# The first weights' transfers on ScalarE's queue, their first half split by ScalarE and VectorE

## The chip, the core and the metric

The kernel runs on one core of one Trainium2 chip. The metric is the device time of the whole program in microseconds (us), less is better. TensorE (PE) does the matmuls and transposes, VectorE (DVE), ScalarE (ACT) and GpSimd (POOL) the elementwise work, SyncE (SP) issues most transfers. All transfers of the core go through 16 DMA engines.

## What is computed

A trunk of two layers over 1024 tokens of width 1024. Cut to what matters here, each layer is:

```python
for l in range(DEPTH):                       # DEPTH = 2
    h = rms_norm(x, norm_g[l])
    proj = h @ w_in[l]                       # [1024, 1024] @ [1024, 2504]
    (qa, ka, va, iq, ik, iw, ga, u, gb, cq, ckv, kpe, gc) = jnp.split(proj, points, axis=-1)
    # three mixers (sparse attention, state-space layer, latent attention), gated
    x = x + mixed @ w_out[l]
```

Only the start of the first layer is touched by the change: the load of x, its norm, and the first of the column groups of `w_in[0]`, the one that gives `ka`, `va`, `ik` and `iw` (128 + 40 + 32 = 200 columns).

## The kernel before

Every matmul operand is held as two fp32r tiles, high part and rest (hi and lo), and a product is three matmuls: hi·hi, hi·lo, lo·hi (lines 758, 760 and 761). Tokens go in eight tiles of 128, named x0 to x7 below, and in two halves (`hf` 0 and 1: x0 to x3, x4 to x7).

Line 703 on, the start: for each token tile a transfer of 512 KB is issued on SP (line 705). After the fourth tile come the constants (line 708), the gains (`load_gains`, lines 671 and 674) and `ws.load(2)`, the first two weight requests: request K for rows 0 to 511 of `w_in` (`kh` 0) and rows 512 to 1023 (`kh` 1). `wload` (line 625) issues one transfer per column range, and K has three ranges (128, 40 and 32 columns), so these are six transfers of 256, 80, 64, 256, 80 and 64 KB, each in 512 rows of 512, 160 or 128 bytes. The names w1 to w6 are used for them below. Then x4 to x7 follow.

`norm_tile` (line 659) takes the squares on ScalarE (line 663), the power −0.5 on GpSimd (`rsq`, lines 162 and 163) and scales on VectorE (line 666). `normed[0]` is the last of these powers. `turn_h` (line 677) transposes four tokens' blocks on TensorE (line 685), takes the high part out of PSUM on ScalarE (line 688, tile `hh`) and the rest on VectorE (line 689, tile `hl`). At line 727 the two weight tiles are split by `split_pool`: high part (line 149) and rest (line 150) on GpSimd, both for 800 columns a partition; `issue_after(normed[0])` holds those of the block's instructions that are on GpSimd behind the last power. `split_act` (line 152) is the other splitter: high part on ScalarE (line 153), rest on the engine that it is given (line 154); it does the splits of all later weights. `proj_halves` (line 737) is the first user: it gets both weight tiles, multiplies tokens x0 to x3 by `kh` 0 and then by `kh` 1 (48 matmuls each), then transposes x4 to x7 and multiplies these.

The order in which each engine runs its instructions is fixed when the program is built: a planner walks the traced program with a timeline of its own and gives each engine, SP included, one queue that runs strictly in order. Where two are ready by the planner's timeline, the one traced earlier goes first. A transfer is an instruction in the queue of the engine that issues it.

Of the kernel before, what the change touches and what calls it, by code (L numbers as in the profile page):

```python
# [86 lines left out]
def hybrid_kernel(ctx, tc, A, out, dbg=None, layers=DEPTH):  # L87
    nc = tc.nc
    V, S, G, T = nc.vector, nc.scalar, nc.gpsimd, nc.tensor
# [9 lines left out]
    def page(shape, dt, name):  # L99
        return pg.tile(shape, dt, tag="pg", name=name)  # L100
# [29 lines left out]
    def f(ap):  # L130
        return ap.bitcast(F32)
# [20 lines left out]
    def split_act(raw, hi, lo, eng=None):  # L152
        S.activation(hi, raw, AF.Copy)  # L153
        (eng or G).tensor_tensor(lo, raw, f(hi), op=ALU.subtract)  # L154
# [444 lines left out]
    class Stream:  # L599
# [20 lines left out]
        def get(self):  # L620
            self.load(LOADS[len(self.reqs) < 9])
            self.split(SPLITS[len(self.reqs) < 9])
            return self.q.pop(0)

    def wload(src, ranges, kh):

        raw = page([128, 4, 256], F32, "raw")
        o = 0
        for c0, c1 in ranges:
            nc.sync.dma_start(raw[:, :, o:o + c1 - c0],  # L630
                              src[512 * kh:512 * kh + 512, c0:c1].rearrange("(k p) c -> p k c", p=128))
            o += c1 - c0
        return raw, o

# [9 lines left out]
    def in_weights(l):  # L644
        cols = dict(K=R_K, I=R_IQ, L=R_L, C=R_CQ, Q=R_QA)
        reqs = []
        for x in "KI" + STEPS:
            if x.isdigit():
                reqs.append(lambda col=GATES[int(x)]: gate_w(l, col))
            elif x == "U":  # L650
                reqs.extend(lambda col=col: gate_w(l, col) for col in (1192, 1320))
            else:
                reqs.extend(lambda r=cols[x], kh=kh: wload(A["w_in"][l], r, kh) for kh in range(2))
        return Stream(reqs)
# [4 lines left out]
    def norm_tile(xt):  # L659

        jk = page([128, 1024], F32, "jk")
        ssq = small(1, "ssq")
        S.activation(jk, xt, AF.Square, accum_out=ssq)
        rst = small(1, "rst")
        normed[0] = rsq(rst, ssq, 1024 * EPS, 1.0 / 1024)
        V.tensor_scalar(jk, xt, rst, None, op0=ALU.mult)
        return jk

    def load_gains(l):
        gp = sm.tile([128, 11], F32, tag="gp", name="gp", bufs=2)  # L670
        nc.sync.dma_start(gp, A["gain_p"][l])
        gr = sm.tile([128, 320], F32, tag="gr", name="gr", bufs=1)
        src = A["gain_r"][l]
        nc.sync.dma_start(gr, bass.AP(tensor=src.tensor, offset=src.offset, ap=[[0, 128], [1, 320]]))
        return gp[:, 0:8], gp[:, 8:10], gp[:, 10:11], gr[:, 0:64], gr[:, 64:128], gr[:, 128:224], gr[:, 224:320]
# [25 lines left out]
    ws = in_weights(0)  # L701
    xnew = []
    for t in range(8):
        xp = page([128, 1024], F32, f"x{t}")
        nc.sync.dma_start(xp, A["x"][0][128 * t:128 * t + 128, :])
        xnew.append(xp)
        if t == 3:
            nc.sync.dma_start(cst_, A["c_all"])
            gains = load_gains(0)
            ws.load(2)  # L710
    htok = [norm_tile(x) for x in xnew[0:4]]
    hT = [[], []]
    turnh = turn_h(0, hT, htok, gains[0])
# [6 lines left out]
    for l in range(layers):  # L720
# [3 lines left out]

        if l == 0:
            with tc.issue_after(normed[0]):
                ws.split(2, split_pool)
        for _ in turnh:
            pass
        h_hi, h_lo = hT  # L730
# [831 lines left out]
        for g in range(2):  # L1562
            if g == 1 and not last:
                ws = in_weights(l + 1)
# [7 lines left out]
            for t in range(8):  # L1572
                cs = slice(128 * t, 128 * t + 128)
                ps = ps_s([128, 512], "po")
                for k in range(8):
                    hi, lo = (w[:, k % 2, :] for w in w_[k // 2][:2])
# [85 lines left out]
```

## Time and profile before

| what | time or share |
|---|---|
| three runs, median (lowest to highest) | 1314.76 us (1314.67 to 1316.2) |
| the profiled execution | 1314.69 us |
| its span | 1312.9 us |
| TensorE busy | 1229.4 us, 94% |
| VectorE, ScalarE, GpSimd busy | 67%, 52%, 52% |
| mean granted TensorE clock | 0.975 of full speed |

The span runs from the first to the last instruction of the profiled execution; the rest of its time lies around it. Times of rows are counted from the span's start. Busy shares are means over the whole program, so what the change is worth is read from the first 40 us alone.

### The profile page before, as it was taken

To read this page: it belongs to the slowest core of one execution; us is meant where nothing else is said; L and a number is where in the kernel's file an instruction comes from. 1 tells how busy PE (TensorE), PEld (TensorE's weight loads), DVE (VectorE), ACT (ScalarE), POOL (GpSimd) and SP (SyncE) were. 2 spreads that over 40 slices of the span, in tenths; PEclk is the share of its full clock that TensorE was granted. 3 is DMA by queue.
4 is the path that set the end of the run, shared out by engine and by line. 5 is a ranking of instruction groups with operands and counts; after the bars stand their busy time and mean duration, and the time that the engine had idled before them with its cause. 6 is when DMAs were issued, how large, how long until landed. Compare 5 with 4: busy or idle time off the path is not lost. (4 is left out here: it accounts for less than half of the span.)

```text
span 1312.9 us, 23852 instructions
## 1 busy us (share of the span) xinstructions
PE 1229.4 (94%) x8644; PEld 1047.7 (80%) x8644; DVE 876.9 (67%) x2342; ACT 686.5 (52%) x1565; POOL 681.0 (52%) x1112
## 2 busy tenths in 40 slices
PE   6898999698999999999999999996989999999998
PEld 6896998487788688877899888975868886887787
DVE  4968889926787787632253887997476879776111
ACT  5256753022778788752143666412157887777300
POOL 5789159767332556313247962795680345643300
PEclk8998999898999999999999999998989999999999
DMA  7011322322300100331140013223303010014102
GB/s 243 15 42 33 103 91 85 113 76 93 86 19 17 43 27 18 108 139 42 80 148 14 21 61 97 73 93 106 117 27 97 7 59 17 12 38 168 70 33 96
DMA packets 78491, 92.79 MB, mean 71 GB/s; under 512 B 13536, under 2 KB 61280, under 8 KB 78368
## 3 DMA queue, kind: packets, MB, share of 16 engines
q1 hardware_dynamic: 77216, 87.03, 20.7%
q0 software_dynamic: 1152, 4.19, 1.0%
q8 instruction: 68, 1.11, 0.4%
q14 instruction: 55, 0.45, 0.1%
HBM read 63.53 MB, written 26.50 MB: 69 GB/s over the span
## 5 line engine op out<-in xcount | busy, mean ns | idle before, releaser
L758 PE MATMUL pj<-whi,hh 128*128 128x256 f32 (+1 forms) x608 | 173.8, 286 | 1.2 <-POOL whi L149 1.2
L760 PE MATMUL pj<-wlo,hh 128*128 128x256 f32 (+1 forms) x608 | 172.6, 284 | 1.6 <-POOL wlo L150 1.6
L761 PE MATMUL pj<-whi,hl 128*128 128x256 f32 (+1 forms) x608 | 172.7, 285 | 0.0
L154 POOL TENSOR_TENSOR wlo<-raw,whi 128x1024 fp32r<-128x1024 f32 (+1 forms) x40 | 96.0, 2412 | 144.0 <-ACT whi L153 123.9
L166 PE MATMUL gt<-hh,whi 128*128 128x512 f32 x320 | 130.7, 408 | 0.0
L168 PE MATMUL gt<-hh,wlo 128*128 128x512 f32 x320 | 129.1, 405 | 0.0
L167 PE MATMUL gt<-hl,whi 128*128 128x512 f32 x320 | 128.8, 403 | 0.0
L760 PEld LDWEIGHTS pj<-wlo,hh 128*128 128x128 f32 x608 | 117.9, 194 | 2.5 <-POOL wlo L150 1.8
L758 PEld LDWEIGHTS pj<-whi,hh 128*128 128x128 f32 x608 | 117.9, 194 | 2.3 <-POOL whi L149 1.4
L761 PEld LDWEIGHTS pj<-whi,hl 128*128 128x128 f32 x608 | 117.7, 194 | 0.3
L1262 ACT ACTIVATE pt<-s 128x512 f32<-128x512 f32 (+1 forms) x154 | 83.4, 555 | 46.0 <-PE s L1256 35.5
L938 DVE SCALAR_TENSOR_TENSOR acc<-rl,iw,acc 128x384 f32<-128x384 f32 (+5 forms) x84 | 93.4, 1114 | 14.9 <-ACT rl L933 11.7
L166 PE MATMUL po<-whi,mix 128*128 128x512 f32 x256 | 98.4, 391 | 1.6 <-DVE gin L1279 1.6
L167 PE MATMUL po<-wlo,mix 128*128 128x512 f32 x256 | 99.7, 390 | 0.0
L168 PE MATMUL po<-whi,mix 128*128 128x512 f32 x256 | 99.6, 390 | 0.0
L1256 PE MATMUL s<-ident,P 128*128 128x128 f32 x588 | 93.9, 276 | 2.0 <-ACT pt L1262 0.7
L1236 ACT ACTIVATE P<-P,nb,asum 128x1024 f32<-128x1024 f32 (+7 forms) x96 | 82.7, 867 | 18.2 <-DVE nb L1234 17.5
L1236 ACT ACTIVATE P<-P,nb,qsc 128x1024 f32<-128x1024 f32 (+7 forms) x96 | 82.4, 865 | 16.5 <-DVE nb L1234 16.5
L1579 DVE TENSOR_TENSOR xn<-xn,po 128x512 f32<-128x512 f32 x32 | 22.0, 688 | 103.3 <-PE po L168 92.0
L1182 ACT ACTIVATE th<-gt 128x512 f32<-128x512 f32 x32 | 19.1, 598 | 134.5 <-PE gt L168 49.1
L933 ACT ACTIVATE rl<-s 128x512 f32<-128x512 f32 (+3 forms) x160 | 74.0, 540 | 23.3 <-PE s L932 16.4
L1228 DVE CUSTOM_DVE_ANT_0 P<-s,bias 128x512 f32<-128x512 f32 (+3 forms) x144 | 76.7, 551 | 13.1 <-PE s L1413 11.3
(451 smaller groups left out, 3597.8 us busy)
## 6 DMA issues: line engine op xcount, KB each, us to landing
raw<-in_w_in SPq DMA_DIRECT2D x32, 512.0 KB, 4.2
gate_d<-gate SPq DMA_DIRECT2D x16, 512.0 KB, 2.9
gin<-gate_d SPq DMA_DIRECT2D x16, 512.0 KB, 4.5
raw<-in_w_out SPq DMA_DIRECT2D x16, 512.0 KB, 5.4
x<-in_x SPq DMA_DIRECT2D x8, 512.0 KB, 5.0
cq_d<-cqs SPq DMA_DIRECT2D x16, 256.0 KB, 2.2
cqT<-cq_d POOLq DMA_DIRECT2D x8, 512.0 KB, 6.3
xn<-in_x SPq DMA_DIRECT2D x8, 512.0 KB, 9.8
```

What stands on the lines that cost most here:

```text
L154: (eng or G).tensor_tensor(lo, raw, f(hi), op=ALU.subtract)
L166: T.matmul(ps, lh, rh, start=start, stop=False)
L167: T.matmul(ps, lh, rl, start=False, stop=False)
L168: T.matmul(ps, ll, rh, start=False, stop=stop)
L758: T.matmul(o, hk, hi[:, k, 0:n], start=kh == 0 and i == 0 and k == 0, stop=False, skip_group_check=True)
L760: T.matmul(o, hk, lo[:, k, 0:n], start=False, stop=False, skip_group_check=True)
L761: T.matmul(o, lk, hi[:, k, 0:n], start=False, stop=kh == 1 and k == 3, skip_group_check=True)
L938: V.scalar_tensor_tensor(a, r[:, 0:nk], w, a, op0=ALU.mult, op1=ALU.add, **({"accum_out": ssum[:, b - 2:b - 1]} if h == 7 else {}))
L1228: V.tensor_tensor_reduce(Ps[j][:, c0:c1], p[:, 0:c1 - c0], bi[:, c0:c1], 1.0, -3.0e38, ALU.add, ALU.max, m)
L1236: S.activation(Ps[j][:, 0:nk], Ps[j][:, 0:nk], AF.Exp, bias=nb[:, j:j + 1], scale=it["scale"][:, j:j + 1], accum_out=sums[:, j:j + 1])
L1256: T.transpose(p[:, i, :], Ps[j][:, 128 * kt:128 * kt + 128], ident)
L1262: S.activation(pt[:, 0:n, :], p[:, 0:n, :], AF.Copy)
```

## The change

The six transfers of the first two weight requests are issued from ScalarE's queue in place of SP's; every later weight request goes by SP again (`issuer`). They are traced ahead of the gains now. The two tiles' high parts are taken on ScalarE in place of GpSimd; the rest of the first tile (`kh` 0) is taken on VectorE and that of the second (`kh` 1) on GpSimd (`ws.q` is empty at the first).

```diff
+    issuer = [nc.scalar]
+
     def wload(src, ranges, kh):
 
         raw = page([128, 4, 256], F32, "raw")
         o = 0
         for c0, c1 in ranges:
-            nc.sync.dma_start(raw[:, :, o:o + c1 - c0],
-                              src[512 * kh:512 * kh + 512, c0:c1].rearrange("(k p) c -> p k c", p=128))
+            issuer[0].dma_start(raw[:, :, o:o + c1 - c0],
+                                src[512 * kh:512 * kh + 512, c0:c1].rearrange("(k p) c -> p k c", p=128))
             o += c1 - c0
         return raw, o
...
         if t == 3:
             nc.sync.dma_start(cst_, A["c_all"])
+            ws.load(2)
+            issuer[0] = nc.sync
             gains = load_gains(0)
-            ws.load(2)
...
         if l == 0:
             with tc.issue_after(normed[0]):
-                ws.split(2, split_pool)
+                ws.split(2, lambda raw, hi, lo: split_act(raw, hi, lo, V if not ws.q else G))
```

## Rows read from the trace of the kernel before

**Rows 1.** The page's busy line: engine, busy us, share, instructions.
```profile
PE 1229.4 (94%) x8644; PEld 1047.7 (80%) x8644; DVE 876.9 (67%) x2342; ACT 686.5 (52%) x1565; POOL 681.0 (52%) x1112
```

**Rows 2.** Stretches of the start: busy us (instructions) of each engine, granted clock, DMA.
```profile
core 0: us, PE busy (x) PEld busy (x) DVE busy (x) ACT busy (x) POOL busy (x), PEclk, DMA share, GB/s
0.00:7.50 7.50, 0.00 (x0) 0.00 (x0) 0.75 (x1) 3.58 (x5) 2.12 (x15) 1.00 0.72 258
7.50:12.90 5.40, 5.33 (x24) 4.09 (x24) 2.26 (x3) 2.85 (x5) 2.31 (x6) 1.00 1.03 298
12.90:16.00 3.10, 0.38 (x2) 0.21 (x2) 2.73 (x4) 1.88 (x4) 2.81 (x3) 0.92 1.06 349
16.00:22.20 6.20, 6.20 (x30) 6.20 (x30) 1.69 (x3) 2.27 (x4) 2.64 (x2) 0.50 1.02 363
22.20:30.50 8.30, 8.30 (x75) 8.30 (x75) 5.57 (x6) 6.83 (x12) 6.37 (x9) 0.99 0.52 120
30.50:38.60 8.10, 6.21 (x55) 5.80 (x55) 8.03 (x17) 4.57 (x8) 7.64 (x18) 1.00 0.24 67
```

**Rows 3.** Timeline, start: start us, us, engine, line, operation [idle before <- releaser].
```profile
0.72 1.28 ACT L663 ACT_TABLE_LOAD   x1 [0.72 <-PEq L1652]
...
4.61 1.06 ACT L663 ACTIVATE jk<-x 128x1024 f32<-128x1024 f32 x1 [2.60 <-DMA x<-in_x]
...
8.83 1.06 ACT L663 ACTIVATE jk<-x 128x1024 f32<-128x1024 f32 x1
...
12.36 0.69 ACT L688 ACTIVATE hh<-tr,gp 128x512 fp32r<-128x512 f32 x1 [2.37 <-PE tr L685]
...
13.10 0.86 POOL L149 TENSOR_SCALAR whi<-raw 128x800 fp32r<-128x800 f32 x1 [1.99 <-DMA raw<-in_w_in]
...
14.02 0.36 PE L758 MATMUL pj<-whi,hh 128*128 128x200 f32 x1 [1.15 <-POOL whi L149]
14.05 1.88 POOL L150 TENSOR_TENSOR wlo<-raw,whi 128x800 fp32r<-128x800 f32 x1
...
15.98 0.53 PE L760 MATMUL pj<-wlo,hh 128*128 128x200 f32 x1 [1.60 <-POOL wlo L150]
```

**Rows 4.** SP's timeline, one window each: issues of w1, w3 to w6, x4 to x7.
```profile
4.55 0.45 SPq L630 DMA_DIRECT2D raw<-in_w_in  x1
...
5.89 1.59 SPq L630 DMA_DIRECT2D raw<-in_w_in  x1
7.56 1.75 SPq L630 DMA_DIRECT2D raw<-in_w_in  x1
9.35 1.84 SPq L630 DMA_DIRECT2D raw<-in_w_in  x1
11.23 0.58 SPq L630 DMA_DIRECT2D raw<-in_w_in  x1
11.85 1.93 SPq L705 DMA_DIRECT2D x<-in_x  x4
```

**Rows 5.** DMA issues, windows 6.5:7.4 (w3), 11.4:11.8 (w6): KB, us from issue to landing.
```profile
raw<-in_w_in SPq DMA_DIRECT2D x1, 64.0 KB, 7.0
...
raw<-in_w_in SPq DMA_DIRECT2D x1, 64.0 KB, 3.3
```

**Rows 6.** DMA by queue, 995.5:997.5 (two queues busy), then 999.5:1001.5 (one): packets, MB, share.
```profile
DMA packets 204, 0.52 MB, mean 260 GB/s; under 512 B 15, under 2 KB 114, under 8 KB 204
...
q0 software_dynamic: 97, 0.37, 72.3%
q1 hardware_dynamic: 107, 0.15, 27.9%
...
DMA packets 221, 0.80 MB, mean 401 GB/s; under 512 B 25, under 2 KB 25, under 8 KB 221
```

**Rows 7.** The later splits by ScalarE and VectorE: duration ns min/median/max, first and last start.
```profile
L153 ACT ACTIVATE whi<-raw x7: 1046/1058/1136, 26.5 to 109.2; 128x1024 fp32r<-128x1024 f32 x7
...
L154 DVE TENSOR_TENSOR wlo<-raw,whi x5: 1212/1222/2146, 63.3 to 113.0; 128x1024 fp32r<-128x1024 f32 x5
```

**Rows 8.** Timeline of TensorE, 30 to 80 us: the rows with a wait.
```profile
31.26 0.33 PE L685 MATMUL tr<-ident,jk 128*128 128x128 f32 x1 [0.25 <-DVE jk L666]
...
35.62 0.66 PE L685 MATMUL tr<-ident,jk 128*128 128x128 f32 x4 [1.65 <-DVE hl L689]
...
62.36 0.41 PE L855 MATMUL tr<-ident,g2k 128*128 128x128 f32 x2 [2.81 <-DVE ka_lo L158]
```

## The prediction

> **What bounds the kernel now.** I read the busy line first: TensorE is busy 94% of the span [rows 1], so an edit pays only where TensorE waits or runs slowly. The change touches the first 40 us, so I read the stretches of the start next [rows 2]. TensorE does nothing until 7.5, is busy 0.38 of the 3.1 us from 12.9 to 16.0, and then works at a granted clock of 0.50 (the 1.2 GHz level) until 22.2: 30 instructions in 6.2 us, 0.207 us each, where the stretch behind it, at 2.4 GHz, does 75 in 8.3 us, 0.111 each. So the gap costs its own length and is followed by a slow stretch that cost 30 × (0.207 − 0.111) = 2.9 us.
>
> The timeline of the start [rows 3] says who ends that gap. ScalarE's first square starts at 4.61 when x0 lands, its fourth at 8.83, and the first eviction `hh` at 12.36. So the token side is ready at 12.36 + 0.69 = 13.05. The first matmul runs at 14.02, behind GpSimd's high part (0.86 us from 13.10, when the weights land); the one behind it at 15.98, behind GpSimd's rest (1.88 us). That is the term the change aims at: 15.98 − 13.05 = 2.9 us, plus the 2.9 us of slow clock behind it.
>
> The weights' own arrival is in the issues [rows 4, 5]: w3, the last piece of `kh` 0, is issued at 5.89 and lands 7.0 us later, at 12.9; w6 at 11.23 + 3.3 = 14.5. SP is held at the issue: 0.45 us when little is queued, 1.59 to 1.84 us for w3 to w5. This holds x4 to x7 back to 11.85. So today's order on the wire is x0 to x3, constants, weights, x4 to x7.
>
> **The sum's base.** The profiled execution took 1314.69 us, the median of the runs is 1314.76: the same. The sum is made against 1314.7. The first projection feeds everything behind it, so I take a shift of its end as a shift of the whole. The next wait of TensorE is at 62.36, 2.81 us for VectorE [rows 8]; VectorE's work ahead of it begins behind the evictions of the second half, so it moves along and is no slack.
>
> **The split, alone.** Removed from GpSimd: two high parts, 2 × 0.86, and one rest, 1.88 [rows 3]. ScalarE takes the high parts: its copy of 1024 columns is 1.058 us, so 800 columns are 0.83. VectorE takes the first rest: 1.222 × 800/1024 = 0.95 [rows 7]. High part and rest would then take 1.8 us in place of 2.7, and ScalarE has 2.37 us idle ahead of its first eviction [rows 3] to hide 2 × 0.83. With weights that land in time this is worth up to the 2.9 + 2.9 us above. VectorE's 0.95 falls where it is busy 2.73 of 3.1 us (12.9 to 16.0) or 1.69 of 6.2 (behind that) [rows 2]; I count it at nothing for the idle 4.5 us of the second, and at 0.95 if it falls into the first.
>
> **The transfers.** Six issues leave SP, so x4 to x7 are issued straight behind the gains, from 4.55 instead of 11.85. On the wire this takes the weights' place ahead of them away. What two busy queues do to each other is shown at 995.5 to 997.5 [rows 6]: queue 0 (rows of 4 KB) sends 97 packets, queue 1 sends 107, of which 15 are tiny, so 92 rows of 1.5 KB. They go about one packet for one, not byte for byte, and together at 260 GB/s where one queue alone made 401. Now count packets for each of the 16 DMA engines: an x tile is 128 rows, 8 each; each of w1 to w6 is 512 rows, 32 each. SP's queue up to x7 has 8 (identity) + 32 + 8 + 8 + 8 (constants, gains) + 32 = 96; `kh` 0 is also 96. One for one, w3 is through about when x7 is. That is 4.9 MB and 0.41 MB; the wire moves 1.94 MB by 7.5 us [rows 2], so at 363 GB/s it begins at 2.2. 5.3 MB at 363 [rows 2] to 260 GB/s end at 17 to 23 us; I take 19, nearer the faster rate because the small rows are only part of the traffic. The next 96 (`kh` 1) run against 1.25 MB of the next weights: 1.66 MB, 4.6 to 6.4 us more, 21 to 29; I take 25. So w3 comes 6 us later than now and w6 10 us.
>
> The Trainium skill (DMA: Bandwidth & Descriptors, Issuing engines are not separate DMA queues) speaks against this part of the change too: transfers from several engines interleave on the same 16 DMA engines and only the issue time is saved. The rows agree as far as the rate goes, 260 against 401 GB/s.
>
> **The issues on ScalarE.** ScalarE's queue is in order and the six issues are ready from the start, so they stand ahead of the squares. At the end of w3's issue (7.48) SP had queued 64 + 96 = 160 packets for each DMA engine and 1.94 MB, some 37 packets, had gone: an issue waits at about 123 outstanding. Taken over to ScalarE's queue, four issues go at once (4 × 0.45 us), the fifth waits until 37 of the weights' packets are through and the sixth until 69. One for one that is 3.5 MB, at 12 to 16 us. The table load, 1.28 us [rows 3], may stand behind. The first square then starts at 12 to 17 instead of 4.61, and queued behind it are all four squares, the powers on GpSimd, the scales and the transposes. From first square to first eviction it is 7.75 us now and about 7.3 with the squares back to back: the token side alone would be ready at 20 to 24. No row shows an issue on ScalarE; the lower bound is the 6 × 0.45 = 2.7 us of unhindered issues, which end before x0 lands and cost nothing.
>
> **The wait that is added.** The two high parts are traced ahead of the evictions, and in the rows ScalarE's queue is in traced order. So the first `hh` stands behind the second high part, which waits for w6: 25.0 + 0.83 = 25.8 instead of 12.36. On GpSimd nothing that TensorE needed stood behind that wait. From there: first matmul at 26.5, then the 107 instructions that stand between 12.9 and 30.5 now [rows 2], 11.9 us at 0.111 each or 14.8 with a slow stretch as today's: end at 38.4 to 41.3 against 30.5, +7.9 to +10.8. The second half gets its tokens early, so today's waits of 0.25 and 1.65 us [rows 8] may go: −1.9 to 0. Sum: +6.0 to +10.8, middle +8.4: **1323.1 us**.
>
> **Rivals.**
> *Weights late, evictions not behind them.* The planner may set the second high part behind the first evictions. Then the token side decides: `hh` at 22, first matmul 22.7, end 34.6 to 37.5, less up to 1.9: +2 to +7, middle 1319. Against it: traced order is what the rows show.
>
> *Weights get two packets for SP's one.* Then w3 passes at SP's 48th packet, 3.1 MB, 11 to 14 us, and w6 at its 96th, 5.7 MB, 18 to 24; the sixth issue ends at 9 to 11, the square starts at 10 to 12.5, `hh` comes at 18 to 25 by both ways. With 20 the end is at 32.6 to 35.5, less 1.9: 0 to +5, about 1316.5. For it stands no row; the 97 to 92 of [rows 6] stand against it. The Trainium skill (DMA: Bandwidth & Descriptors, Queues, rings and completion order) has the DMA engines change queues only after a whole packet, typically some 9 to 17 descriptors; that would lean this way for the weights' many small rows.
>
> *Weights early, the gain is had: faster.* If ScalarE's queue is served first, or by bytes, the six transfers' 0.82 MB take 2.7 us at 298 GB/s [rows 2] and are in by some 6 us; no issue is held, x0 is late by at most 2.7 us. Both high parts fit into ScalarE's idle 2.37 us. The first matmul goes at 13.9 to 15.7, nothing waits for a rest, and the 107 instructions take 11.9 to 14.8: end at 25.8 to 30.5, −4.7 to 0, and −1.9 more at best; about 1312. It decides on one thing: w6 landed before some 13 us. For it: the weights now enter the wire at once, not behind constants and gains.
>
> *Nothing reaches the end.* Later waits take up what the start does: 1314.7. The order of later work may also be planned anew; no row prices that, and I leave 2 us for it in the ends of the range.
>
> **How the numbers follow.** Likeliest, 0.50: weights late and evictions behind them, 1323.1, its own range 1319 to 1330. Evictions not behind: 0.14. Two for one: 0.10. Faster: 0.21. Nothing: 0.05. About 0.2%, 2.6 us, is what a measurement can tell from no change. Slower by more: 0.50 + three quarters of 0.14 + 0.4 of 0.10 = 0.64; within: 0.15; faster by more: 0.21. The range takes in most of the faster case (1310.8) and the late one up to 1330.5.
>
> **What would show it.** Right: packets of two queues at once in the first 25 us; w6 landed after 20; ScalarE's first square after 10; its first `hh` after 20, its idle time ended by the weights' transfer; TensorE's second half starting 6 us or more later. Wrong: the first square still near 5, w6 landed by 13, the first two matmuls of line 758 and 760 close together before 16, no stretch at 0.50 behind them. The forecast falls first if the two queues don't go one for one, then if ScalarE is not held at its issues.

## The result: 0.57% slower, the forecast time by another sum

| | before | after |
|---|---|---|
| median of the runs, us | 1315.18 (1313.2 to 1320.21) | 1323.09 (1322.59 to 1323.99) |
| after to before | | 1.0057, 95% interval 1.0044 to 1.007 |
| profiled execution, us (span) | 1314.69 (1312.9) | 1322.59 (1320.8) |
| first `hh` on ScalarE, us | 12.36 | 20.52 |
| first projection matmul, us | 14.02 | 21.25 |
| end of the first phase, us | 30.5 | 34.3 |

The profile after, its busy line, to be held against [rows 1]: every engine's busy time is within 0.5% of before's.

```profile
PE 1231.0 (93%) x8644; PEld 1050.4 (80%) x8644; DVE 878.3 (66%) x2343; ACT 686.6 (52%) x1567; POOL 677.9 (51%) x1109
```

The stretches of the start after, cut at its own events (columns as in [rows 2]).

```profile
0.00:14.50 14.50, 0.00 (x0) 0.00 (x0) 0.75 (x1) 4.18 (x6) 2.35 (x15) 1.00 0.92 301
14.50:21.20 6.70, 5.49 (x24) 4.65 (x24) 4.76 (x4) 3.58 (x8) 4.64 (x7) 1.00 1.06 376
21.20:23.00 1.80, 1.80 (x11) 1.75 (x9) 1.77 (x3) 1.73 (x4) 0.00 (x0) 1.00 1.15 245
23.00:34.30 11.30, 11.30 (x104) 11.30 (x103) 8.20 (x10) 8.97 (x15) 6.34 (x9) 1.00 0.20 49
```

TensorE begins 7 us later, at 14.5 in place of 7.5 [rows 2]. The granted clock of 1.00 in the first three stretches is no reading: this trace has no record of the clock before 23.0, and the column then shows 1.00 (in before the records begin at 12.1, so the same holds for the first of [rows 2]). The starts of TensorE's instructions lie 0.21 us apart up to 23.0, as at 1.2 GHz. Behind that, the stretch from 23.0 to 34.3 does 104 instructions in 11.3 us, 0.109 each, the pace of 2.4 GHz. Before, 30 instructions went 0.207 apart up to 22.2 [rows 2].

The timeline of the start after (columns as in [rows 3]; ACTq are the issues of ScalarE's queue, first to last).

```profile
0.72 9.56 ACTq L632 DMA_DIRECT2D raw<-in_w_in  x6
10.31 1.28 ACT L665 ACT_TABLE_LOAD   x1 [10.31 <-issue]
11.61 1.06 ACT L665 ACTIVATE jk<-x 128x1024 f32<-128x1024 f32 x1
...
14.74 1.04 ACT L665 ACTIVATE jk<-x 128x1024 f32<-128x1024 f32 x1
15.78 1.62 ACT L153 ACTIVATE whi<-raw 128x800 fp32r<-128x800 f32 x2
...
20.52 0.69 ACT L690 ACTIVATE hh<-tr,gp 128x512 fp32r<-128x512 f32 x1 [3.12 <-PE tr L687]
...
21.25 0.54 PE L761 MATMUL pj<-whi,hh 128*128 128x200 f32 x1
21.59 0.41 PE L763 MATMUL pj<-wlo,hh 128*128 128x200 f32 x1
```

ScalarE's queue stands at its six issues until 10.28; table load, squares and all that hangs on them follow. The two high parts run without a wait at 15.78: the weights had landed. The first `hh` waits for TensorE's transposes, not for weights. And the first two matmuls are 0.34 us apart instead of 1.96 [rows 3]: the wait for the rest, at which the change aims, is gone, but 7 us later than it was met before.

What held ScalarE is not in a view but in the records of its DMA issues. Every transfer of SP and of ScalarE reports its landing on one of eight semaphores, given out in turn, and its issue waits until the transfer that had the semaphore before has landed:

```
transfer  issued at  waits for the landing of
w1        0.72       -
w2        1.22       -
w3        5.90       x0
w4        8.79       x2
w5        9.20       w1
w6        9.76       w2
x4 (SP)  10.08       x3
```

So w3 and w4 wait for token tiles that SP had sent first, and everything queued behind them on ScalarE waits too. SP's queue shows the same waits in a view, the waits of SP's queue up to 14 us (us in total, times, longest):

```profile
SPq L676 <- DMA x<-in_x: 3.0, 1, 3.0
SPq L707 <- DMA x<-in_x: 2.2, 1, 2.2
SPq L707 <- DMA consts<-in_c_all: 1.0, 1, 1.0
```

x4's issue at 10.08 dates x3's landing: some 1.2 us later than the 8.83 at which the fourth square could start before [rows 3]. The fourth square itself starts at 14.74. Of its 5.9 us, 1.2 are x3's later landing, with the weights on the wire beside the tokens, and the other 4.7 are the held queue.

How the two queues shared the wire is in the DMA view of after from 2 to 6 us (packets, MB, share of the 16 engines' time; q1 is SP's queue, and q10, which before does not have, is ScalarE's). Both had work all along: by the records w2 landed at 7.66 and x3 at 10.06.

```profile
q1 hardware_dynamic: 307, 0.93, 62.9%
q10 hardware_dynamic: 1040, 0.34, 38.4%
```

More than three packets of the weights went for one of SP's, not one for one; in after's second profile it was 1028 to 298.

**Where the 7.9 us are.** I followed each TensorE instruction from one trace to the other (same line, same tile, same occurrence) and took the median difference of their starts over a stretch. These are worked out, not rows. The two last columns are second profiles, of before and of after, against the first profile of before.

| stretch of before, us | after | before again | after again |
|---|---|---|---|
| 0 to 10 | +7.0 | +0.1 | +7.5 |
| 20 to 34 | +3.2 | −1.0 | +4.4 |
| 300 to 320 | +1.6 | −1.8 | +6.1 |
| 370 to 385 | +2.6 | −1.6 | +6.5 |
| 410 to 430 | +7.6 | −1.6 | +9.9 |
| 600 to 640 | +7.0 | −0.2 | +9.3 |
| 1280 to the end | +7.9 | +0.7 | +10.0 |

The shift comes in two portions: one at the start, and a second between 375 and 410 us, in attention of layer 0, where no line was edited.

### The profile page after: what moved, and what is told of

Same layout as the page of the kernel before. It is cut to its first block, busy times and chain, and to the rows that moved or that the text cites. A ratio compares the mean times of both kernels' runs of the same rounds, so it can differ in the third digit from the quotient of the medians.

```text
span 1320.8 us, 23855 instructions
## 1 busy us (share of the span) xinstructions
PE 1231.0 (93%) x8644; PEld 1050.4 (80%) x8644; DVE 878.3 (66%) x2343; ACT 686.6 (52%) x1567; POOL 677.9 (51%) x1109
## 3 DMA queue, kind: packets, MB, share of 16 engines
q0 software_dynamic: 1152, 4.19, 1.0%
q10 hardware_dynamic: 3168, 0.82, 0.3%
## 5 line engine op out<-in xcount | busy, mean ns | idle before, releaser
L1229 DVE TENSOR_SCALAR_CACHE_REDUCE P<-s 128x512 f32<-128x512 f32 (+3 forms) x144 | 74.4, 550 | 16.5 <-PE s L1393 11.4
```

What stands on the lines that cost most here:

```text
L1229: V.tensor_scalar(Ps[j][:, c0:c1], p[:, 0:c1 - c0], 1.0, -3.0e38, op0=ALU.mult, op1=ALU.max, accum_out=m)
```

## Experiments

Two theories. **D** (the step on record): the start's delay passes whole to the end. **O**: the second portion is the order of instructions, which the builder plans anew for any edit. Other tiny edits to the start also make the planner choose the order of before or that of after, and that separates start from order.

**Order of after, start of before.** Before, with the identity matrix issued by GpSimd:

```
-    nc.sync.dma_start(ident, A["c_ident"])
+    nc.gpsimd.dma_start(ident, A["c_ident"])
```

> The kernel before with one line changed: the identity matrix (64 KB, the first transfer of the program) is issued by GpSimd's queue in place of SP's. All tokens and all weights stay on SP, and GpSimd splits the weights as in before, so the start should stand as in before: squares from about 4.6 us or 0.4 earlier, first hh at 12 to 12.4, the first phase's end at 30 to 30.5. But the list of instructions, planned anew by the program's builder for any edit, is from then on that of the changed kernel: the same order on TensorE and, but for one instruction, on VectorE. Theory D (the step on record: the start's delay passes whole to the end, the later order costs nothing): no delay, so 1314 to 1315.5 us, ratio 0.999 to 1.0005. Theory O (the start's delay is used up by 300 us to some 1.6 us, and the rest comes of the order in the stretch from 375 to 410 us): the shift against before is within 1 us of zero at 300 us, +4 to +7 after 410 us, and the end 1319 to 1323, ratio 1.003 to 1.006.

Measured: 1319.31, ratio 1.0032 (1.0021 to 1.0043). The profiled execution, the shortest of its seven, is 3.2 us ahead of before at 20 to 34 us, 4.3 ahead at 300, level at 410 and 1.8 behind at the end. So the order costs some 4 us with no delay at the start (the medians are 4.0 apart); D's 1314 to 1315.5 is out.

**Start of after, that stretch in the order of before.** After, with x0's transfer cut in two halves of columns:

```
-        nc.sync.dma_start(xp, A["x"][0][128 * t:128 * t + 128, :])
+        for j in range(2 if t in (0,) else 1):
+            w = 512 if t in (0,) else 1024
+            nc.sync.dma_start(xp[:, w * j:w * j + w], A["x"][0][128 * t:128 * t + 128, w * j:w * j + w])
```

> The changed kernel with the first token tile's transfer cut in two halves of columns, and nothing else. The start should stand as in the changed kernel: ScalarE's six issues held until about 10, squares from about 11.6, first hh at 20 to 21, the first phase's end at 34 to 35 (+3.5 to +4.5). The order of VectorE's instructions between 320 and 430 us comes out as in the kernel before (6 differing rows in that tenth in place of 228), and after the middle of the program as in the changed kernel. Theory D (the start's delay passes whole): 1322 to 1324 us, ratio 1.005 to 1.007, as the changed kernel. Theory O (the order between 375 and 410 us costs some 6 us): +1 to +2.5 at 300 us, the same at 430 us, and the end 1315.5 to 1318, ratio 1.0005 to 1.0025.

Measured: 1319.65, ratio 1.0035 (1.0019 to 1.0051); the shift is +4.0 at 20 to 34, +4.3 at 300, +4.4 at 410 to 430, +4.6 at the end. Flat: no step at 375 to 410, and the start's delay passes whole. The time is above what O expected, since nothing was taken up by 300 us. The start was also not that of after: one transfer more moves the turn of the semaphores, the sixth issue waited until 12.35, for w2's landing, and now the step on record did happen, `hh` behind a high part behind the weights:

```profile
0.72 12.03 ACTq L632 DMA_DIRECT2D raw<-in_w_in  x6
...
20.93 0.87 ACT L153 ACTIVATE whi<-raw 128x800 fp32r<-128x800 f32 x1 [1.83 <-DMA raw<-in_w_in]
21.71 0.67 ACT L690 ACTIVATE hh<-tr,gp 128x512 fp32r<-128x512 f32 x1
```

**The same pair on another queue.** After, with the weights issued by GpSimd's queue:

```
-    issuer = [nc.scalar]
+    issuer = [nc.gpsimd]
```

> The changed kernel with the first weights' six transfers issued by GpSimd's queue in place of ScalarE's; split by ScalarE and VectorE and GpSimd as in the changed kernel. Later order of instructions: TensorE's but for 7 rows and VectorE's wholly as in the changed kernel. Theory H (ScalarE's compute was late because its queue stood at its own issues until tokens 0 and 2 had landed): without these the table load stands at 0.7 again, the squares begin at 4.6 to 6.5 (tokens share the wire with the weights at most), first hh at 12.4 to 16, the first phase's end at 30 to 33. The rival (packets of two queues share the wire, tokens themselves late): tokens land 3 us later or more and the squares begin at 8 or later. Theory D: the end is before's plus the first phase's own shift, 1314 to 1318. Theory O: the end is that of the order alone, 1319.5 to 1322.5, ratio 1.0035 to 1.0055, whatever the start.

Then the same with the identity brought in two halves of rows, which gives the order of before:

```
-    nc.sync.dma_start(ident, A["c_ident"])
+    for j in range(2):
+        nc.sync.dma_start(ident[64 * j:64 * j + 64], A["c_ident"][64 * j:64 * j + 64])
```

> The run before this one with the weights on GpSimd's queue (e4), and one edit more: the identity matrix is brought in two halves of 64 rows. That edit hardly touches the start, but the order planned for the rest comes out as in the kernel before: TensorE's in every row, VectorE's and ScalarE's in all but one. Both have one start, so they differ in the order alone. If the order from 375 to 410 us costs some 4 us (theory O): the three waits of TensorE there (1.0, 1.5 and 0.6 us, found in all three kernels with the changed order) are gone, no step of the shift against before in that stretch, end 1316 to 1318, ratio 1.000 to 1.0025, some 4 to 5 us under e4. If the order is innocent and the loss of e4 is of its start: 1321 to 1323, ratio 1.004 to 1.006, the step of 4 us somewhere else or there all the same.

Measured: 1321.99, ratio 1.0049 (1.0036 to 1.0062), and 1318.21, ratio 1.0024 (1.0012 to 1.0036). At 20 to 34 us they are +1.9 and +1.8; from 370 to 430 the first goes from +1.7 to +5.1, the second stays at +1.7. Each against its own runs of before (1315.29 and 1315.14), the first is 6.7 us over and the second 3.1: the order alone is worth 3.6 us here, 3.4 in the profiles. The two starts are not one in detail (first square at 4.93 and 7.26, first `hh` at 18.13 and 19.64), but level from 20 us on. The waits of TensorE from 370 to 410 us, in the trace of before, of after (the first of this pair shows the same three lines) and of the second of this pair:

```profile
PE s L1256 <- DVE mx L1228: 0.3, 1, 0.3
```

```profile
PE acc_o L1252 <- DVE gin L1282: 1.5, 1, 1.5
PE s L1415 <- DVE mx L1231: 1.0, 1, 1.0
PE s L507 <- DVE mx L1231: 0.6, 1, 0.6
```

```profile
PE s L1260 <- DVE mx L1232: 0.3, 1, 0.3
```

3.1 us against 0.3, to the tenth the same for one order whatever the start (the run with the identity on GpSimd's queue has the three waits too, the one with x0 in two pieces the 0.3). The first of them in after's timeline of VectorE and TensorE: the score matmul waits for a buffer whose reader on VectorE stands behind a scan of 2.12 us.

```profile
380.78 2.12 DVE L490 TENSOR_TENSOR_SCAN s5z<-s5rho,s5z 128x512 f32<-128x512 f32 x1
382.83 0.66 DVE L1231 CUSTOM_DVE_ANT_0 P<-s,bias 128x512 f32<-128x512 f32 x1
...
383.55 0.50 PE L1415 MATMUL s<-ka_hi,qA 128*128 128x512 f32 x1 [1.02 <-DVE mx L1231]
```

The waits make 2.8 us of the step. It is 3.4 us here, 4.3 with the identity on GpSimd's queue and in after's second profile, and 5.9 in after's first, where the granted clock fell as well (0.96 from 372 to 410, against 1.00 in the second). The rest I have not followed.

As to the start, the queue on GpSimd frees ScalarE, as expected of the held queue: table load at 0.72, first square at 4.93. But the tokens do come late there, so the rival has a part too, and `hh` at 18.13 is past the 16 that was allowed. Squares in the first of the pair:

```profile
4.93 1.06 ACT L665 ACTIVATE jk<-x 128x1024 f32<-128x1024 f32 x1 [2.93 <-DMA x<-in_x]
...
12.53 1.06 ACT L665 ACTIVATE jk<-x 128x1024 f32<-128x1024 f32 x1 [1.73 <-DMA x<-in_x]
```

The fourth waits for x3 until 12.53; before it was 8.83 [rows 3]. So with no hold, and the weights on GpSimd's queue, the tokens' part alone reaches 3.7 us; in after the whole is 5.9. The one is not to be taken off the other: on GpSimd's queue the six transfers went in 320 packets (1472 on that queue in place of 1152), on ScalarE's in 3168, and three of x4 to x7 were issued as early as 4.72 to 6.34.

**Transfers alone.** After, with the split of before:

```
-                ws.split(2, lambda raw, hi, lo: split_act(raw, hi, lo, V if not ws.q else G))
+                ws.split(2, split_pool)
```

> The six transfers moved to ScalarE's queue as in the changed kernel, but both halves split by GpSimd, as in before. The start's ScalarE rows should stand as in the changed kernel up to the squares (table load at about 10.3, squares from 11.6), and first hh at 17.5 to 20.6, since it waits there for TensorE's transposes and not for the split; the first phase's end 33.5 to 35. The later order is almost that of the changed kernel. If the transfers alone make the start late: as the changed kernel, 1321 to 1324 us, ratio 1.0045 to 1.0075. If the split on ScalarE and VectorE has a part of the loss: 1 to 2 us less.

Measured: 1323.29, ratio 1.0058 (1.0046 to 1.007): the change's whole loss, and the split has no part in it. TensorE's first transpose is at 14.59 (14.53 in after). At 20 to 34 us, though, the shift is only +1.8 (after: +3.2 and +4.4): `hh` comes at 19.56, and the matmuls go 0.11 us apart from about 21, in after from 23.0. The medians show nothing of it, so a start's shift in one profile is not the shift of the time to better than some 2 us.

**Split alone.** Before with the line of the split changed, and in the first of two runs also the constants brought in two pieces, for an order close to before's:

```
-                ws.split(2, split_pool)
+                ws.split(2, lambda raw, hi, lo: split_act(raw, hi, lo, V if not ws.q else G))
```
```
-            nc.sync.dma_start(cst_, A["c_all"])
+            nc.sync.dma_start(cst_[:, 0:512], A["c_all"][:, 0:512])
+            nc.sync.dma_start(cst_[:, 512:949], A["c_all"][:, 512:949])
```

> The split alone, all transfers on SP as in before: both high halves on ScalarE, the low ones on VectorE and GpSimd. Beside it the constants' transfer is cut in two, for which the order of the rest comes out nearly as in before (2 differing rows in place of 228 in the fourth tenth on VectorE). Squares from about 4.6 as in before; the two high halves stand on ScalarE ahead of the first hh and wait for the last weights at 13, so first hh 14.5 to 15.5 (12.4 in before), first projection matmul 15 to 16 (14.0), but the second one no longer waits 1.6 us for a low half on GpSimd: 15.3 to 16.3 (16.0); the first phase's end within 1 us of before. The split on ScalarE and VectorE costs nothing: 1313.5 to 1316.5, ratio 0.999 to 1.001. If the high halves ahead of hh pass on whole: +2, 1317, ratio 1.0015.

> The split alone again, without the cut of the constants' transfer: the same start as in e10, but an order of the rest that is neither that of before nor that of the changed kernel (34 differing VectorE rows in the fourth tenth, 68 and 123 in the eighth and ninth). Theory D (only the start counts): the same as e10 within 0.1%. Theory O (every order has its own price): it may differ from e10 by up to 6 us either way, with a step of the shift in the stretches where the orders differ (from 320 to 430 us and from 900 to 1180 us); no number before the run.

Measured: with the order close to before's 1315.7, ratio 1.001 (0.9996 to 1.0024), no difference; with the third order 1317.74, ratio 1.0018 (1.0007 to 1.0029). The second had a start 0.8 us later (first `hh` at 16.13 against 15.36) but was 0.4 us ahead of it from 345 to 560 us; its loss comes behind 960, from −1.1 to +2.0, where the orders differ. About 1 us of that is a fall of the clock near 1203, and the rest is not traced to its waits. The two high parts on ScalarE end the wait for a rest on GpSimd and start another: 2.5 us for `hh` in the first, in TensorE's waits up to 40 us:

```profile
PE pj L759 <- ACT hh L688: 2.5, 1, 2.5
```

**Weights first.** After, with the weights traced ahead of the token loop:

```
     ws = in_weights(0)
+    ws.load(2)
+    issuer[0] = nc.sync
     xnew = []
...
-            ws.load(2)
-            issuer[0] = nc.sync
             gains = load_gains(0)
```

> The changed kernel with the weights' six transfers put ahead of the token loop in the program: ScalarE's queue issues four of them without any wait, and the last two wait for the two first small transfers and no longer for tokens; SP sends the tokens behind the identity, the constants and the gains. The order of the rest is that of before nearly everywhere. Theory H (ScalarE was held because its issues waited for tokens to land): its last issue is done by 3 to 6 us in place of 10.3, the table load follows, the squares wait for the tokens, which land behind 0.8 MB of weights: squares from 6 to 8.5, first hh at 14.5 to 17, the first phase's end 31 to 34. If the hold came of the six issues themselves, not of what they wait for: table load again at about 10, squares from 11.6, hh at 20. Time, by the order of before and +1 to +3 at the start: 1315.5 to 1318.5, ratio 1.0005 to 1.0025; a start that is earlier than before's: 1313 to 1315.

Measured: 1321.16, ratio 1.0039 (1.0024 to 1.0053), above what was expected. The hold is as theory H of the run on GpSimd's queue has it, by which ScalarE stands because its issues wait for landings:

```profile
0.73 5.57 ACTq L632 DMA_DIRECT2D raw<-in_w_in  x6
6.33 1.28 ACT L665 ACT_TABLE_LOAD   x1 [6.33 <-DMA raw<-in_w_in]
10.77 1.06 ACT L665 ACTIVATE jk<-x 128x1024 f32<-128x1024 f32 x1 [3.16 <-DMA x<-in_x]
```

With no token to wait for, the issues end 4 us earlier. But now the tokens' issues on SP wait for the weights' landings (x0 goes at 4.14), the first square is at 10.77 and `hh` at 18.62, 1.6 later than I allowed. The shift is +3.6 at 20 to 34 and +3.5 up to 560, while the median is 6.0 over before. In part this is the clock: the profiled execution lost 1.3 near 565 and 2.7 near 1203 as TensorE's clock fell. What other executions lost I cannot tell. Waits and stretch at 1203, of this run, then of before:

```profile
PE s L1391 <- ACT pt L1265: 1.8, 1, 1.8
1200.00:1224.00 24.00, 22.22 (x174) 0.86 0.29 100
```

```profile
1200.78 0.44 PE L1388 MATMUL s<-kc0h,qT 104*128 104x384 f32 x1 [1.73 <-ACT pt L1262]
...
1195.00:1216.00 21.00, 19.17 (x163) 1.00 0.30 108
```

The same wait of 1.7 to 1.8 us of an idle TensorE, and behind it a granted clock that fell in one execution (0.86 over the stretch) and not in the other (1.00).

**A start that is better.** Before, with the constants put behind the first weights, the orders of all engines but SP unchanged; then the split alone (with the constants in two pieces) with the same move:

```
-            nc.sync.dma_start(cst_, A["c_all"])
             gains = load_gains(0)
             ws.load(2)
+            nc.sync.dma_start(cst_, A["c_all"])
```

> The kernel before with the constants' transfer (486 KB) put behind the first weights on SP's queue in place of ahead of them; the order of every instruction on TensorE, VectorE and ScalarE is that of before. A try for a start that beats both kernels: the weights stand 486 KB further ahead, which at the 300 to 400 GB/s of that stretch is 1.2 to 1.6 us. High half on GpSimd from 11.5 to 11.9 (13.1 in before), low half done at 14.4 to 14.8, so the second projection matmul at 14.4 to 14.8 (15.98), the first phase's end 29 to 29.5 where TensorE's pace is as in before. If an earlier start passes to the end: 1313.5 to 1314.3 us, ratio 0.999 to 1.000, hardly to be told from before. If the constants are then late for their first reader: a wait for them near 24 us and 1315 to 1317.

> The split alone (e10) with the constants' two transfers behind the weights as well. First high half on ScalarE at 11.4 to 11.8 (13.04 in e10), first hh at 13.8 to 14.2 (15.36), first projection matmul about 14.1 and the second right behind it (15.98 in before), so the first phase's end 1 to 2 us earlier than in e10. If the start passes to the end: 1312.5 to 1315 us, ratio 0.998 to 1.0. If the granted clock's falls, which come in other places in every execution, outweigh it: 1314 to 1317, as e10.

Measured: 1313.51, ratio 0.9984 (0.9972 to 0.9995), and 1312.94, ratio 0.9977 (0.9962 to 0.9993). Both are faster than both kernels, by 0.16% and 0.23% against before; one is not to be told from the other. GpSimd's high part in the first, then the split and the first two matmuls in the second:

```profile
11.83 0.86 POOL L149 TENSOR_SCALAR whi<-raw 128x800 fp32r<-128x800 f32 x1
```

```profile
11.75 0.87 ACT L153 ACTIVATE whi<-raw 128x800 fp32r<-128x800 f32 x1 [1.15 <-DMA raw<-in_w_in]
13.39 0.87 ACT L153 ACTIVATE whi<-raw 128x800 fp32r<-128x800 f32 x1 [0.76 <-DMA raw<-in_w_in]
14.16 0.67 ACT L688 ACTIVATE hh<-tr,gp 128x512 fp32r<-128x512 f32 x1
...
14.88 0.36 PE L759 MATMUL pj<-whi,hh 128*128 128x200 f32 x1 [0.99 <-ACT hh L688]
15.08 0.28 PE L761 MATMUL pj<-wlo,hh 128*128 128x200 f32 x1
```

The weights are there 1.3 us earlier than the 13.10 of [rows 3], as worked out, and the second matmul runs at 15.02 in the first (later than the 14.8 allowed) and at 15.08 in the second, in place of 15.98. At 20 to 34 us the two stand 4.0 and 3.7 us ahead of the first profile of before; most of it is that the matmuls go 0.11 us apart there from the first on, with no stretch at 0.50. At the end of the profiles 0.2 and 2.5 us are left.

**Second profiles** of both kernels, for what belongs to the program and what to the execution:

> The kernel before once more, for a second profile. In the first one TensorE ran its matmuls 0.21 us apart (half pace, granted clock 0.50) from 16 to 22 us, which hides some 3 us of the changed kernel's delay at the first phase's end (+3.8 in place of +8.2 at the first hh). If the fall belongs to this kernel's start: again 0.50 from about 16 to 22. If it comes by chance: the clock stays at 1.00 there as in the run with the identity on GpSimd's queue, the first phase ends about 3 us earlier, and the difference to the changed kernel at that point is 6 to 7 us.

> The changed kernel once more, for a second profile. By theory: ScalarE's six issues again last until about 10 us, squares from 11 to 12, first hh 20 to 21, three waits of TensorE from 375 to 410 us of 1.0, 1.5 and 0.6 us. Those are of the program and should come again to within 0.1 us; the falls of the granted clock (38 to 46 us, 390 to 405 us) may come in other places and shift the rows behind them by 1 to 3 us.

Measured: 1315.41 and 1324.71. Stretch 14 to 22 of before, first profile, then second (busy us and instructions of TensorE, granted clock, DMA share, GB/s):

```profile
14.00:22.00 8.00, 6.38 (x30) 0.59 1.02 371
```

```profile
14.00:22.00 8.00, 6.48 (x38) 1.00 1.03 371
```

The second 1.00 is no reading up to 20.0, where the records of the clock begin in that trace: its matmuls lie 0.21 us apart until 20.0 and 0.11 behind. In the first they lie 0.11 apart from 12.1 to the gap, 0.21 from 16 to 22.3 and 0.11 behind. So both starts had a slow pace, which ended 2.3 us earlier in the second, and neither expectation is met in full. In after's second profile the issues last until 10.83, `hh` comes at 20.93, and the three waits at 375 to 410 are 1.0, 1.5 and 0.6 again. Its +6.1 at 300, where the first had +1.6, goes in part with falls of the granted clock in other places: the second profile has one of 6.8 us at 124.1, the first profile none there.

## Why the forecast was right, and where its working was wrong

**Kept as right.** ScalarE's queue is held and the squares stand behind it: forecast 12 to 17 for the first, measured 11.61, just under it, and 12.16 in the second profile. Token side ready at 20 to 24: first `hh` at 20.52 and 20.93, though from first square to first `hh` it took 8.9 and 8.8 us and not the 7.3 on record. Table load behind the issues: 10.31. The split alone costs nothing: 1.001 (0.9996 to 1.0024). Both directions of cause hold, transfers bad, split harmless.

**Wrong: what holds the queue.** The step said an issue waits at about 123 outstanding packets. The records show waits for landings, of x0 and of x2, on reused semaphores; where the turn of the semaphores changes, the hold moves (the sixth issue starts at 9.76 in after, at 12.35 with x0 in two pieces, at 5.92 with the weights first). Once nothing was left to wait for, each issue on ScalarE took 0.38 to 0.53 us in after. SP's issues in before wait for landings too: by the records w3 starts at 5.89 and w4 at 7.56, right behind the landings of x1 (5.85) and x2 (7.54). But the 1.59 to 1.84 us of [rows 4], from which I made the limit, count from those starts, so these waits do not explain them; whether they are a limit of packets stays open. The step's 12 to 16 for the sixth issue is 10.28 in the trace; that the squares came out near is luck, two different waits that end at like times. The Trainium skill (DMA: Bandwidth & Descriptors, Anatomy of one DMA — SWDGE (gpsimd) path) says that any semaphore wait of a transfer is done by the issuing sequencer before dispatch. The records agree: it is ScalarE's sequencer that stands from 1.75 to 5.90. And its rule that issuing from several engines saves only issue time (same page of the Trainium skill, Issuing engines are not separate DMA queues) was still too kind here: the SP time saved was paid with 9.6 us of ScalarE.

**Wrong: one packet for one, and with it the weights at 19 and 25.** The forecast was to fall first if the two queues don't go one for one, and they went 1040 to 307. The last pieces of the weights were issued at 5.90 and 9.76 and landed some 6.3 and 5.5 us later, at 12.2 and 15.3. So the wait for w6 ahead of `hh` (25.8 on record) is not there, the first matmul is at 21.25 and not 26.5, and the first phase is late not by 8.4 us but by 3.2 and 4.4 at 20 to 34 us in the two profiles of after, where before's second stands at −1.0. x4 to x7, which were to compete with the weights, waited for x3 and went at 10.08. Three of the signs set for right did not come: w6 landed after 20, `hh` held by the weights' transfer, and the second half 6 us later (its first transpose is at 33.74 and 34.95, in before at 30.52 and 29.50). The case that I put at 0.14, evictions not behind the weights with +2 to +7, is what the start did, though by early weights and not by the planner's order. The case at 0.10, two packets for one, had its rows as well: w3 at 11 to 14, sixth issue ended by 9 to 11, first square 10 to 12.5, `hh` 18 to 25, end 32.6 to 35.5, all but w6; its time, 1316.5 (the middle of its 0 to +5 would be 1317.2), was without the order.

**Wrong: nothing else changes.** I named a new order of later work and left 2 us for it in the ends of the range. It is a term of the sum: 3.6 us (GpSimd's queue, both orders), 4.0 (order of after, start of before). The start's share is then the rest of 7.9, about 4; a start as late at 20 to 34 us (+4.0, x0 in two pieces), with that stretch in the order of before, measured 4.4 (1319.65). 4 + 4 gives the forecast's +8.4 nearly, and that is chance: one term was twice too large, the other left out.

**Right, with a reservation: the shift passes to the end.** With the order of before it does: +4.0, +4.3, +4.4, +4.6 along the program, and +3.6 and +3.5 up to 560 with weights first. In single executions falls of the clock add or take 1 to 4 us on the way. The medians are over these shifts, by 0.4 us with x0 in two pieces, 1.3 on GpSimd's queue with the order of before and 2.4 with the weights first; before's second profile, ahead by 1.0 at 20 to 34 us, would account for 1.0 of each.

**Not shown: the 2.9 us of slow clock as the gap's price.** With the first matmuls 0.34 us apart, after still went 0.21 us from one to the next until 23.0. The split got none of the up to 2.9 + 2.9 us that the step gave it for weights in time: with the weights 1.3 us earlier, 1312.94 with the split and 1313.51 without are not to be told apart.

**Not settled:** why the planner chooses one order or the other (several small edits of the start's transfers turned it), what is left of the step beyond the three waits, and what fills SP's long issues in before.

## To carry to other kernels

A transfer that is moved to an engine's own queue brings along what its issue waits for; look up the transfer that last used its completion semaphore before you put an issue ahead of that engine's work. Where the order of instructions is planned by the builder, compare the two orders far behind the edit, and use a small edit that gives the same order as a control: here about half of the difference was order. What is not needed yet (here the constants) goes behind what is.

## What the runs showed that I had not expected

- Eight completion semaphores in turn couple SP's and ScalarE's queues: w3 on ScalarE waited for x0 on SP until 5.90, x0 on SP for w1 on ScalarE until 4.14 when the weights went first. The six transfers issued by GpSimd waited for none of these.
- Two profiles of one program differ by up to 4.5 us in the middle (after at 300 us: +1.6 and +6.1) and by 2.1 at the end. The granted clock falls behind the same waits in one execution and not in another.
- The granted clock's column shows 1.00 where a trace has no record of the clock: before 12.1 and 20.0 in the two profiles of before, before 23.0 and 18.3 in those of after. The pace there is that of 1.2 GHz: after's first projection matmuls go 0.21 us apart from 21.59 to 22.02, with 1.00 in the column for 21.2 to 23.0.
